# Lane inversions from VectorE to GpSimd, and the second half's statistics cut into three stages

## The chip, the cores and the metric

The kernel runs on one core of a Trainium2 chip. The metric is the device time of one launch in microseconds (us). The engines are named as in the profile: PE is TensorE's matmul side and PEld its weight load, DVE is VectorE, ACT is ScalarE, POOL is GpSimd, SP is SyncE, which issues the DMAs of this kernel. Each engine works through its own queue in order, and waits on semaphores that other engines and DMAs raise. Differences under 0.2% of the time (2.8 us) count as no change.

## The reference, cut to what matters

One layer of a hybrid decoder on x of 1024 tokens by 1024 channels, float32. The mixer normalises x, multiplies it by one projection, and splits the columns among a gated unit (A), a recurrent block (B) and RWKV-7 time mixing (C); then comes the output projection, and a gated feed-forward network with a final norm. What matters here is C, whose state is updated token by token:

```
def step(state, inp):
    r_t, w_t, k_t, v_t, kk_t, a_t = inp
    sa = jnp.einsum('bhvk,bhk->bhv', state, kk_t)
    state = (state * w_t[:, :, None, :]
             - sa[..., :, None] * (kk_t * a_t)[..., None, :]
             + v_t[..., :, None] * k_t[..., None, :])
    return state, jnp.einsum('bhvk,bhk->bhv', state, r_t)
```

and the norm in front of the mixer:

```
y = xf * lax.rsqrt(jnp.mean(xf * xf, axis=-1, keepdims=True) + EPS)
```

## The kernel before

The tokens are done in two halves of 512. For each half the six heads of C are done as three pairs, so there are six units of time mixing, called 00, 10, 20, 01, 11 and 21 (pair, half). Every product with a weight is three matmuls of 512 columns per 128 rows of the contraction (high and low parts of weight and activation, `gemm`).

The step above is done in chunks of 64 tokens. Within a chunk it needs the inverse of a triangular 64x64 matrix. One unit has 8 chunks and 2 heads, so 16 such matrices, and its work is cut into stages:

- `P` (function `rwkv`, up to its last `yield`): projections of k, r and v, then the matmuls `pg` (L624), from which DVE writes the matrices into `AK` (L628); SP stores them to the scratch `dA` in DRAM (L637).
- `L` (function `lanes`): SP loads the 64 diagonal 16x16 blocks of the unit back as `LA` (L668), one block to a partition; 15 steps of elimination follow, each a product into `LT` (L673) and a subtraction from `LX` (L675), on 8 to 36 elements a partition, and a negation (L676). These 31 instructions, each of which needs the one before, are called a lane here. SP stores the result (L679) and loads the whole matrices back into `AK` (L682).
- `M` (function `chain`): four DVE transposes `X` (L695), the matmuls `pz` and `py` (L690), which put the 16x16 inverses together to 64x64, and then the 8 chunks one after the other (matmuls `q`, L743).
- `E` (function `finish`): norm, gate and store of the unit's output `o`, with the transposes `po` (L783) on PE.

Beside them stand `B` and `R` (the recurrent block), `U` (the gated unit, whose values `pzt`, `sv` and gates `pu` appear below), `X` (inputs `xwa`, `xg`), `M` without digits (`macc`: one block of the modulation vector, multiplied on ACT and added on POOL), `S` (function `stats1`: sums of squares of the second half, their matmuls `pss`, the reciprocal root `rsq_n` on DVE, and its broadcast `pb_n` on PE, L266) and `H1` (the normalised second half, `h10` to `h17`). After the mixer come the output projection (`out_tile`, matmuls into `po`, L246 to L248) and the feed-forward network.

The order of the stages is the text `ORDER`: each word calls the next stage of a generator. Inside that, a scheduler that runs when the kernel is built orders the instructions of each engine by its own idea of when each can start; so a change of an instruction's engine also moves others. The engine for many elementwise steps comes from the table `ENG` through `eng()`; the lane is not in it. Of the PSUM pool `mp` there are three buffers, which `pss`, `pb`, `pg`, `pzt`, `pix`, `pz` and others take in turn.

Three names for stretches of PE's program: a unit's head runs from its last `pg` to its first `pz`, and holds the lane and the DMAs around it; its body runs from there to the next unit's last `pg`; behind the sixth `pz` comes the tail, up to the transposes `po` of unit 21.

Of the kernel before, what the change touches and what calls it, by code (L numbers as in the profile page):

```python
# [14 lines left out]
ALU = mybir.AluOpType  # L15
# [3 lines left out]
P = 128  # L19
D = 1024  # L20
S = 1024
# [100 lines left out]
H2N = (4, 4)  # L122
MODN = 10
XB = 2
ORDER = """X0*2 P00*3 S L00 B00 M U0 L00 M U0 M R00
M00*3 P10 M00 P10 M M00 P10 L10 M E00 R00 U0 M R00 E00 L10 B10 M R00 U0
M10*3 P20 M10 P20 M M10 P20 L20 M E10 R10*2 M E10 B20 R10*2 L20 M R20*4
M20 H1*2 M20*2 H1*2 X1 M X1 P01 M20 P01 M M20 P01 L01 M E20*2 L01 B01 M U1 R01
# [21 lines left out]
def trunk(ctx: ExitStack, tc: tile.TileContext, xT, wmod, w_in, w_out, w_up, w_down,  # L150
          par, const, sgu_ln, sgu_wT, sgu_b, lora, g2w, lruw, outT):
    nc = tc.nc
    V, A, G, T = (Ordered(tc, e) for e in (nc.vector, nc.scalar, nc.gpsimd, nc.tensor))
# [56 lines left out]
    def rsqrt(v, n, nm):  # L210

        t = cp.tile([P, 3, 16], F32, tag="rsq", name=f"rsq_{nm}", bufs=3)
        y, h, u = t[:, 0, 0:n], t[:, 1, 0:n], t[:, 2, 0:n]
        yi = y.bitcast(I32)
        V.tensor_single_scalar(yi, v.bitcast(I32), 1, ALU.arith_shift_right)
        V.tensor_scalar(yi, yi, -1.0, float(0x5F3759DF), ALU.mult, ALU.add)
        V.tensor_scalar(h, v, -0.5, None, ALU.mult)
        for _ in range(3):
            V.tensor_tensor(u, y, y, ALU.mult)
            V.tensor_tensor(u, u, h, ALU.mult)  # L220
            V.scalar_tensor_tensor(y, u, 1.5, y, ALU.add, ALU.mult)
        return y

    def eng(key, d):
        return {"V": V, "G": G, "A": A}[ENG.get(key, d)]
# [21 lines left out]
            T.matmul(ps, hi[k], al, start=False, stop=False)  # L247
            T.matmul(ps, lo[k], ah, start=False, stop=(k == len(acts) - 1))  # L248

    def sumsq_bcast(acc, psp, pool, tag, nm, bufs, direct=False):  # L250

        pss = psp.tile([P, H], F32, tag="m", name=f"pss_{nm}")
        for i, a in enumerate(acc):
            for j in range(4):
                T.matmul(pss[:, j:j + 1], a[:, j * P:(j + 1) * P], ones, start=(i == 0 and j == 0),
                         stop=(i == len(acc) - 1), skip_group_check=True)
        return rstd_bcast(pss, psp, pool, tag, nm, bufs, direct)

    def rstd_bcast(pss, psp, pool, tag, nm, bufs, direct=False):

        v = cp.tile([P, 4], F32, tag="rsv", name=f"rsv_{nm}", bufs=2)
        V.tensor_scalar(v, pss[:, 0:4], 1.0 / D, EPS, ALU.mult, ALU.add)
        r = rsqrt(v, 4, nm)
        pb = psp.tile([P, H], F32, tag="m", name=f"pb_{nm}")
        for j in range(4):
            T.matmul(pb[:, j * P:(j + 1) * P], r[:, j:j + 1].broadcast_to([P, P]), ident, start=True, stop=True)  # L266
        if direct:
            return pb
        rb = pool.tile([P, H], F32, tag=tag, name=f"rb_{nm}", bufs=bufs)
        A.copy(rb, pb)  # L270
        return rb
# [30 lines left out]
    mp = ctx.enter_context(tc.tile_pool(name="mp", bufs=3, space=PSUM))  # L302
# [27 lines left out]
    with tc.tile_pool(name="st", bufs=1, reuse_waits="tile") as st:  # L330
# [88 lines left out]
        mod_load(1)  # L419
        mod_ap(0)  # L420
        rb = sumsq_bcast([sacc], mp, st, "rb", "n10", 1)
        mod_v(0, 0, 8)
        w_load(0)
# [29 lines left out]
    r2 = r2s.enter_context(tc.tile_pool(name="r2", bufs=1, reuse_waits="tile"))  # L453
# [62 lines left out]
    def t2(nm):  # L516
        return r2.tile([P, H], F32, tag="t2", name=nm, bufs=NT2)

    def tb(nm):
        return r2.tile([P, H], F32, tag="tb", name=nm, bufs=NTB)  # L520
# [5 lines left out]
    def c_tile(f, wi, idx, o, nm):  # L526

        if f == 0 and wi in first:
            ps = first[wi]
        else:  # L530
            wt = load_w(w_in[wi], f"{nm}{f}")
            ps = acp.tile([P, H], F32, tag="acc", name=f"pc_{nm}{f}")
            gemm(ps, wt, acts[f])
        mu = col("rwkv_mu", idx)
        A.activation(o, ps, AF.Copy, scale=omu[:, idx:idx + 1])
        V.scalar_tensor_tensor(o[:, 1:H], ps[:, 0:H - 1], mu, o[:, 1:H], ALU.mult, ALU.add)
        if f == 0:
            A.copy(cryC[:, idx:idx + 1], ps[:, H - 1:H])
        else:
            V.scalar_tensor_tensor(o[:, 0:1], cryC[:, idx:idx + 1], mu, o[:, 0:1], ALU.mult, ALU.add)  # L540
        return o
# [5 lines left out]
    def rwkv(j, f, stages):  # L547
# [67 lines left out]
        r = c_tile(f, 3 + 3 * j, j, t2(f"r{n}"), f"r{j}")  # L615
# [35 lines left out]
        v = c_tile(f, 4 + 3 * j, 6 + j, t2(f"v{n}"), f"v{j}")  # L651
# [9 lines left out]
        def lanes():  # L661

            LA = r2.tile([P, 16, 16], F32, tag="LA", name=f"LA{n}", bufs=2)
            LX = r2.tile([P, 8, 16], F32, tag="LX", name=f"LX{n}", bufs=2)
            LT = r2.tile([P, 128], F32, tag="LT", name=f"LT{n}", bufs=1)
            blk = dA.rearrange("c h (b x) -> (c h b) x", x=1040)[:, 0:1024].rearrange("u (s t) -> u s t", t=64)
            for qq in range(2):
                SY.dma_start(LA[64 * qq:64 * qq + 64], blk[:, 0:16, 0:16])  # L668
            eng("lx", "G").tensor_copy(LX.rearrange("p a b -> p (a b)"), ey)
            for i in range(15):  # L670
                m, w = i // 2 + 1, 15 - i
                tmp = LT[:, 0:m * w].rearrange("p (a b) -> p a b", b=w)
                V.tensor_tensor(tmp, LX[:, 0:m, i:i + 1].broadcast_to([P, m, w]),  # L673
                                LA[:, i:i + 1, i + 1:16].broadcast_to([P, m, w]), ALU.mult)
                V.tensor_tensor(LX[:, 0:m, i + 1:16], LX[:, 0:m, i + 1:16], tmp, ALU.subtract)  # L675
            V.tensor_scalar(LX, LX, -1.0, None, ALU.mult)  # L676
            yield
            for qq in range(2):
                SY.dma_start(blk[:, qq:16:2, 0:16], LX[64 * qq:64 * qq + 64])  # L679
            for hh in range(2):  # L680
                r_ = slice(64 * hh, 64 * hh + 64)
                SY.dma_start(AK[r_, :, 0, r_], dA[:, hh, 0:4096].rearrange("c (s t) -> s c t", t=64))  # L682
            yield
# [83 lines left out]
        def finish():  # L767
# [28 lines left out]
            yield  # L796

        stages.update({f"L{j}{f}": lanes(), f"M{j}{f}": chain(), f"E{j}{f}": finish()})
        yield

# [136 lines left out]
    rb1 = []  # L937

    def stats1():

        acc = r2.tile([P, H], F32, tag="o", name="sacc", bufs=1)
        for k in range(KT):
            x = tb(f"xs1{k}")
            SY.dma_start(x, xT[k * P:(k + 1) * P, H:S])
            A.activation(acc if k == 0 else x, x, AF.Square)
            if k:
                eng("st1", "G").tensor_tensor(acc, acc, x, ALU.add)
        rb1.append(sumsq_bcast([acc], mp, r2, "rb", "n11", 1))
        yield

    def h1_in():
# [9 lines left out]
    def x_in(f):  # L961
# [14 lines left out]
        yield  # L976

    stages = {"M": mods(), "S": stats1(), "H1": h1_in()}
    for f in range(2):
        stages[f"X{f}"] = x_in(f)  # L980
# [4 lines left out]
    V.on = VPIN > 0  # L985
    for nw, w in enumerate(ORDER.split()):
        if nw == VPIN:
# [60 lines left out]
    def h2_in(f, acc):  # L1048

        rb = sumsq_bcast(acc, mp, f1, "rb", f"n2{f}", 1)  # L1050
        yield
        hn = x1[f]
        sh = [modc[:, 24 + k:25 + k] for k in range(KT)]
        for q in range(4):
            for i, new in enumerate((hnew, hnew) if f == 0 else (anew, gnew)):
                k = q + 4 * i
                V.scalar_tensor_tensor(hn[k], hn[k], sg2[:, k:k + 1], rb, ALU.mult, ALU.mult)
                parts(f"{i + 1}{f + 1}", q, hn[k], new, sh[k])
                yield
        for q in range(4 * f):  # L1060
            b11, b21, b12, b22 = x1[0][q], x1[0][q + 4], hn[q], hn[q + 4]
            eng("T1", "V").tensor_tensor(b11, b12, b11, ALU.subtract)
            eng("T3", "G").tensor_tensor(b12, b22, b12, ALU.subtract)
            eng("T2", "V").tensor_tensor(b22, b22, b11, ALU.subtract)
            eng("T4", "G").tensor_tensor(b21, b21, b22, ALU.subtract)
            parts("T2", q, b22, anew, sh[q + 4])
            parts("T1", q, b11, anew)
            parts("T4", q, b21, gnew)
            yield
        for q in range(4 * f):  # L1070
            parts("T3", q, hn[q], anew, dsh[:, q:q + 1])
            yield
# [227 lines left out]
    for f in range(2):  # L1300
        acc = f1.tile([P, H], F32, tag="g0", name=f"sa3{f}", bufs=NAHEAD + 1)
# [102 lines left out]
```

## Time and profile before

| | us |
|---|---|
| median of 3 runs (1388.76 to 1389.72) | 1389.36 |
| the profiled execution's own time | 1389.59 |
| its span in the profile | 1387.8 |
| PE busy | 1256.2 (91%) |
| DVE busy | 914.4 (66%) |
| ACT busy | 584.0 (42%) |
| POOL busy | 413.3 (30%) |

The mixer and the modulation fill the first 600 us, the output projection runs to about 642 us, and the rest is the feed-forward network. PE is busy nearly everywhere, but a row's duration on PE also holds what the clock costs: the granted clock (PEclk) is 1.00 where TensorE has its higher level of 2.4 GHz, and 0.50 at 1.2 GHz; a stretch's mean lies between. In the section of rows below, the seven windows of the first group are, from the top: body 20, head 01, head 11, head 21, the tail, the stretch behind the tail, and the output projection.

### The profile page before, as it was taken

The numbers are of one execution on the slowest core, as the hardware profiler recorded it, in microseconds if no ns is written. First come the engines' busy times: TensorE is split into PE (matmuls) and PEld (weight loads), VectorE is DVE, ScalarE is ACT, GpSimd is POOL, SyncE is SP. The second block draws the span as 40 slices with busy tenths as digits, with TensorE's granted clock in tenths as the row PEclk, the third lists the DMA queues.
The fourth block names the chain that finished last, engine by engine and source line by source line (L and its number), as shares of the span: only waits on it lengthen the run. The fifth ranks groups of instructions, "written<-read, shape, count | busy, mean of one in ns | idle before, by whom it ended". The sixth has DMA issues, their size and how long they took to land. (4 is left out here: it accounts for less than half of the span.)

```text
span 1387.8 us, 18658 instructions
## 1 busy us (share of the span) xinstructions
PE 1256.2 (91%) x6948; PEld 1025.9 (74%) x6948; DVE 914.4 (66%) x1624; ACT 584.0 (42%) x1008; POOL 413.3 (30%) x337
## 2 busy tenths in 40 slices
PE   2778999978898979989878999999999999999996
PEld 2566878667686867768656778888888888888885
DVE  7968776765668584567898766666666575332566
ACT  3454654854655366333444334343343342110231
POOL 5683423306124220023466433323333200000000
PEclk9999999979999988899989999999999999999998
DMA  6554161433314243385412322222222374321213
GB/s 225 189 168 121 35 168 52 113 126 97 83 51 109 65 124 107 116 272 188 137 45 84 100 91 84 91 84 91 74 71 91 109 261 133 93 76 51 82 54 121
DMA packets 87498, 153.89 MB, mean 111 GB/s; under 512 B 37616, under 2 KB 39280, under 8 KB 87408
## 3 DMA queue, kind: packets, MB, share of 16 engines
q1 hardware_dynamic: 87408, 152.71, 35.3%
q8 instruction: 54, 0.88, 0.3%
q14 instruction: 36, 0.29, 0.1%
HBM read 126.60 MB, written 26.08 MB: 110 GB/s over the span
## 5 line engine op out<-in xcount | busy, mean ns | idle before, releaser
L1246 DVE SCALAR_TENSOR_TENSOR x<-pd,modc,x 128x512 f32<-128x512 f32 x80 | 59.5, 748 | 83.4 <-PE pd L248 83.3
L1293 POOL TENSOR_TENSOR x<-x,rb_n 128x512 f32<-128x512 f32 x2 | 3.0, 1520 | 218.2 <-ACT rb_n L270 218.2
L287 POOL TENSOR_TENSOR macc<-macc,wm 128x512 f32<-128x512 f32 x35 | 46.8, 1338 | 68.1 <-ACT wm L285 66.0
L228 ACT CAST wh_wd<-wr_wd 128x768 fp32r<-128x768 f32 (+2 forms) x32 | 21.7, 677 | 93.6 <-PE pd L247 92.2
L229 POOL TENSOR_TENSOR wl_wo<-wr_wo,wh_wo 128x1024 fp32r<-128x1024 f32 x9 | 22.0, 2445 | 113.3 <-DVE O L774 57.6
L1224 POOL TENSOR_TENSOR u<-u,g 128x512 f32<-128x512 f32 x21 | 27.7, 1321 | 92.6 <-ACT g L1147 92.6
L229 DVE TENSOR_TENSOR wl_ug<-wr_ug,wh_ug 128x1024 fp32r<-128x1024 f32 x22 | 28.9, 1318 | 34.3 <-ACT wh_ug L228 34.3
L755 DVE TENSOR_SCALAR U<-q,rn 128x64 f32<-128x64 f32 x48 | 13.4, 279 | 48.3 <-PE q L743 41.1
L624 PE MATMUL pg<-KGd,KB 128*128 128x128 f32 x192 | 31.1, 307 | 7.5 <-DVE KGd L609 5.0
L763 ACT COPY O<-q 128x64 f32<-128x64 f32 x48 | 10.1, 211 | 65.5 <-PE q L743 65.2
L228 ACT CAST wh_ug<-wr_ug 128x1024 fp32r<-128x1024 f32 x22 | 23.1, 1052 | 34.2 <-PE pA L1122 31.3
L743 PE MATMUL q<-SS,KGd 128*128 128x64 f32 x180 | 36.7, 287 | 0.0
L743 PE MATMUL q<-VV,SCd 128*128 128x64 f32 x192 | 35.0, 285 | 0.3
L1208 DVE TENSOR_TENSOR p<-p,pB 128x512 f32<-128x512 f32 x21 | 14.4, 685 | 31.0 <-PE pB L1123 31.0
L1147 ACT ACTIVATE g<-g 128x512 f32<-128x512 f32 x44 | 27.9, 634 | 14.8 <-DVE g L1142 14.8
L624 PEld LDWEIGHTS pg<-KGd,KB 128*128 128x128 f32 x192 | 27.2, 215 | 9.0 <-DVE KGd L609 5.7
L228 ACT CAST wh_wo<-wr_wo 128x1024 fp32r<-128x1024 f32 x16 | 16.7, 1047 | 38.8 <-PE po L247 30.9
L743 PEld LDWEIGHTS q<-VV,SCd 128*128 128x128 f32 x192 | 29.9, 202 | 4.1 <-ACT O L763 1.4
L1140 DVE SCALAR_TENSOR_TENSOR g<-pA,pr,g 128x511 f32<-128x511 f32 (+1 forms) x42 | 31.2, 742 | 2.4 <-ACT g L1138 2.2
L1140 DVE SCALAR_TENSOR_TENSOR g<-p,pr,g 128x511 f32<-128x511 f32 (+1 forms) x42 | 32.1, 764 | 0.9 <-ACT g L1138 0.9
L285 ACT ACTIVATE wm<-wm,cs 128x512 f32<-128x512 f32 x35 | 24.1, 718 | 15.3 <-DMA wm<-in_wmod_dram 9.3
L1201 POOL TENSOR_TENSOR wr_ug<-wr_ug,wr_uv 128x512 f32<-128x512 f32 x18 | 29.7, 1651 | 1.4
(5041 smaller groups left out, 4574.1 us busy)
## 6 DMA issues: line engine op xcount, KB each, us to landing
wm<-in_wmod_dram SPq DMA_DIRECT2D x48, 512.0 KB, 4.1
wr_ug<-in_w_up_dram SPq DMA_DIRECT2D x22, 512.0 KB, 3.6
wr_uv<-in_w_up_dram SPq DMA_DIRECT2D x22, 512.0 KB, 3.6
wr_g<-gd SPq DMA_DIRECT2D x22, 512.0 KB, 3.5
x<-in_xT_dram SPq DMA_DIRECT2D x32, 256.0 KB, 5.2
wr_wo<-in_w_out_dram SPq DMA_DIRECT2D x16, 512.0 KB, 4.3
wr_wd<-in_w_down_dram SPq DMA_DIRECT2D x16, 384.0 KB, 3.0
gd<-c SPq DMA_DIRECT2D x21, 256.0 KB, 2.0
```

The lines of the kernel that those rows point to most:

```text
L228: A.copy(hi, src)
L229: (e or V).tensor_tensor(lo, src, hi.bitcast(F32), ALU.subtract)
L285: A.activation(acc if k == 0 else wt[:, j, :], wt[:, j, :], AF.Copy, scale=cs[:, k:k + 1])
L287: G.tensor_tensor(acc, acc, wt[:, j, :], ALU.add)
L624: T.matmul(pg[hh][:, c, :, :], KB[:, 4 * g + c, :, :].rearrange("p a b -> p (a b)"), KG[g][:, c, :, r_], start=True, stop=True)
L743: T.matmul(o, w, x, start=start, stop=True, skip_group_check=True)
L1140: V.scalar_tensor_tensor(g[:, d:H], src[:, 0:H - d], taps[2 - d], g[:, d:H], ALU.mult, ALU.add)
L1147: A.activation(g, g, AF.Silu)
L1201: eng("S4" + e, "G").tensor_tensor(g1, g1, v1, ALU.subtract)
L1208: V.tensor_tensor(self.p1, self.p1, psB, ALU.add)
L1224: eng("c22", "V").tensor_tensor(u3, u3, g1_, ALU.mult)
L1246: V.scalar_tensor_tensor(x, ps, modc[:, 40 + k:41 + k], x, ALU.mult, ALU.add)
```

## The change

The 31 instructions of each lane go from DVE to POOL, 186 in all. `stats1`, until now one stage, becomes three: the sums; the matmuls `pss` with the reciprocal root; the broadcast. In `ORDER` the single `S` becomes three, and the first goes behind the first `L00`. For this the function `rstd_bcast` is cut, and `sumsq_col` holds its first part.

```
-ORDER = """X0*2 P00*3 S L00 B00 M U0 L00 M U0 M R00
+ORDER = """X0*2 P00*3 L00 S B00 M U0 L00 S M U0 M S R00
...
-    def sumsq_bcast(acc, psp, pool, tag, nm, bufs, direct=False):
+    def sumsq_col(acc, psp, nm):

         pss = psp.tile([P, H], F32, tag="m", name=f"pss_{nm}")
...
-        return rstd_bcast(pss, psp, pool, tag, nm, bufs, direct)
-
-    def rstd_bcast(pss, psp, pool, tag, nm, bufs, direct=False):
-
         v = cp.tile([P, 4], F32, tag="rsv", name=f"rsv_{nm}", bufs=2)
         V.tensor_scalar(v, pss[:, 0:4], 1.0 / D, EPS, ALU.mult, ALU.add)
-        r = rsqrt(v, 4, nm)
+        return rsqrt(v, 4, nm)
+
+    def sumsq_bcast(acc, psp, pool, tag, nm, bufs, direct=False):
+
+        return rstd_bcast(sumsq_col(acc, psp, nm), psp, pool, tag, nm, bufs, direct)
+
+    def rstd_bcast(r, psp, pool, tag, nm, bufs, direct=False):
+
         pb = psp.tile([P, H], F32, tag="m", name=f"pb_{nm}")
...
-                V.tensor_tensor(tmp, LX[:, 0:m, i:i + 1].broadcast_to([P, m, w]),
+                G.tensor_tensor(tmp, LX[:, 0:m, i:i + 1].broadcast_to([P, m, w]),
                                 LA[:, i:i + 1, i + 1:16].broadcast_to([P, m, w]), ALU.mult)
-                V.tensor_tensor(LX[:, 0:m, i + 1:16], LX[:, 0:m, i + 1:16], tmp, ALU.subtract)
-            V.tensor_scalar(LX, LX, -1.0, None, ALU.mult)
+                G.tensor_tensor(LX[:, 0:m, i + 1:16], LX[:, 0:m, i + 1:16], tmp, ALU.subtract)
+            G.tensor_scalar(LX, LX, -1.0, None, ALU.mult)
...
-        rb1.append(sumsq_bcast([acc], mp, r2, "rb", "n11", 1))
+        yield
+        sums = sumsq_col([acc], mp, "n11")
+        yield
+        rb1.append(rstd_bcast(sums, mp, r2, "rb", "n11", 1))
         yield
```

What this does to PE's program: counted in matmuls of 512 columns, the six heads held 105, 112, 90, 107, 117 and 91, and hold 98, 102, 86, 72, 86 and 84 now. The five bodies held 46, 50, 108, 56 and 40, and hold 49, 68, 109, 63 and 64. In the tail stand 87 such matmuls where there were 58, and 12 more are left behind it. The head of unit 01, on PE, before (`pz01` is its first `pz`, `pc_r11` and `pc_k11` are projections of the next unit):

```order
L247 MATMUL pc_r11_3526<-h14l_2659,wh_r11_3522 128x512
L248 MATMUL pc_r11_3526<-h14h_2658,wl_r11_3521 128x512
L690 MATMUL pz01_3238<-X101_3232,AKd1_122 32x16 x32
L246 MATMUL pc_r11_3526<-h15h_2665,wh_r11_3522 128x512
L247 MATMUL pc_r11_3526<-h15l_2666,wh_r11_3522 128x512
```

and now:

```order
L246 MATMUL pc_k11_3418<-h11h_2579,wh_k11_3414 128x512
L247 MATMUL pc_k11_3418<-h11l_2580,wh_k11_3414 128x512
L693 MATMUL pz01_3238<-X101_3232,AKd1_122 32x16 x32
L248 MATMUL pc_k11_3418<-h11h_2579,wl_k11_3413 128x512
L246 MATMUL pc_k11_3418<-h12h_2586,wh_k11_3414 128x512
```

The `pz` that stood behind 14 of the 24 products of r now stands behind 5 of the 24 products of k, 35 matmuls of the head earlier.

On POOL the end of the first lane, now (`wl_k` is the low part of the weight of k for unit 10, `macc` the modulation, `LX_2219` the identity for a later lane, `wl_r` the low part of r's weight):

```order
L678 TENSOR_TENSOR LX_745<-LX_745,LT_746 128x7x3
L229 TENSOR_TENSOR wl_k_1198<-wr_k_1197,wh_k_1199 128x1024
L676 TENSOR_TENSOR LT_746<-LX_745,LA_744 128x14
L678 TENSOR_TENSOR LX_745<-LX_745,LT_746 128x7x2
L676 TENSOR_TENSOR LT_746<-LX_745,LA_744 128x8
L678 TENSOR_TENSOR LX_745<-LX_745,LT_746 128x8
L679 TENSOR_SCALAR LX_745<-LX_745 128x128
L290 TENSOR_TENSOR macc_852<-macc_852,wm_3_1375 128x512 x2
L672 COPY LX_2219<-cst 128x128
L229 TENSOR_TENSOR wl_r_1306<-wr_r_1305,wh_r_1307 128x1024
```

One wide product has got into the lane, and the POOL work that stood free before waits behind its end. In the same way two additions to `macc` stand inside the lane of unit 01, and one wide product in that of unit 11.

On SP the store and load behind the lane of unit 11, before:

```order
L679 DMA dA11_3587<-LX11_3696 64x8x16 x2
L523 DMA yd_108<-xr01_3174 128x512
L281 DMA wm9_1_4488<-in_wmod_dram 128x1024
L682 DMA AKd0_121<-dA11_3587 64x8x64 x2
L238 DMA wr_xr21_4508<-in_w_in_dram 128x1024
```

and now:

```order
L682 DMA dA11_3587<-LX11_3696 64x8x16
L685 DMA AKd0_121<-dA11_3587 64x8x64
L526 DMA yd_108<-o01_3855 128x512
L685 DMA AKd0_121<-dA11_3587 64x8x64
L238 DMA wr_v21_4368<-in_w_in_dram 128x1024
```

Two transfers that stood between store and load are gone, and one store of an earlier unit's output has come between the halves of the load. For units 10 and 21 nothing stands between any more (before: two transfers each); for unit 20 the load of the weight of `xg` does.

## Rows read from the trace of the kernel before

**Rows 1.** Windows: length; PE, PEld, DVE, ACT, POOL busy (count); PEclk; DMA share; GB/s.
```profile
277.30:344.30 67.00, 52.41 (x450) 44.44 (x449) 40.52 (x70) 34.42 (x62) 21.02 (x18) 0.85 0.35 113
344.30:381.00 36.70, 32.55 (x156) 24.86 (x154) 23.60 (x75) 22.85 (x39) 7.19 (x5) 1.00 0.33 85
413.20:458.80 45.60, 39.94 (x192) 30.83 (x193) 33.68 (x105) 20.50 (x38) 19.52 (x12) 0.93 0.45 120
487.60:531.10 43.50, 36.31 (x182) 27.89 (x180) 35.71 (x91) 26.17 (x45) 7.39 (x3) 0.88 0.43 120
531.10:578.60 47.50, 43.97 (x388) 36.25 (x387) 22.32 (x54) 23.68 (x46) 2.41 (x1) 0.78 0.28 89
578.60:598.80 20.20, 12.43 (x54) 9.40 (x54) 11.38 (x18) 9.60 (x17) 0.00 (x0) 0.95 0.78 251
598.80:641.70 42.90, 42.42 (x184) 34.42 (x184) 25.45 (x35) 11.70 (x15) 12.21 (x5) 0.95 0.74 246
```

**Rows 2.** Waits of PE, 60 to 620 us: in total, times, longest.
```profile
PE po L783 <- DVE LX L675: 5.3, 3, 4.0
PE pb_n L266 <- DVE rsq_n L221: 3.6, 1, 3.6
```

**Rows 3.** Windows of the six lanes, first to last instruction, all work (columns of rows 1).
```profile
115.60:127.20 11.60, 8.02 (x29) 6.49 (x28) 10.84 (x42) 4.80 (x7) 4.95 (x3) 0.71 0.29 93
184.00:197.50 13.50, 13.19 (x70) 10.33 (x70) 13.19 (x56) 7.88 (x12) 0.00 (x0) 1.00 0.45 137
253.20:264.80 11.60, 11.05 (x48) 8.18 (x48) 10.89 (x52) 10.60 (x15) 2.07 (x2) 1.00 0.17 50
355.40:371.80 16.40, 13.38 (x62) 9.74 (x60) 14.89 (x58) 10.12 (x17) 2.60 (x2) 1.00 0.32 101
426.90:447.20 20.30, 15.00 (x72) 11.72 (x71) 20.30 (x76) 8.66 (x13) 9.86 (x6) 0.98 0.32 105
500.30:520.20 19.90, 12.71 (x49) 8.93 (x50) 19.62 (x63) 14.04 (x20) 5.49 (x2) 0.78 0.38 133
```

**Rows 4.** Timeline of POOL: start, us, instruction; each needs the one before.
```profile
68.67 0.20 POOL L146 TENSOR_TENSOR spt<-spt 128x3 f32<-128x3 f32 x1
68.96 0.23 POOL L146 TENSOR_SCALAR spt<-spt 128x3 f32<-128x3 f32 x1
```

**Rows 5.** Timeline, POOL and DVE side by side inside the first lane.
```profile
117.64 2.34 POOL L229 TENSOR_TENSOR wl_k<-wr_k,wh_k 128x1024 fp32r<-128x1024 f32 x1 [2.71 <-ACT wh_k L228]
117.69 2.33 DVE L675 TENSOR_TENSOR LX<-LX,LT 128x24 f32<-128x24 f32 x1
```

**Rows 6.** The same windows, instructions that touch LT alone.
```profile
115.60:127.20 11.60, 9.72 (x30) 0.71 0.29 93
184.00:197.50 13.50, 5.44 (x30) 1.00 0.45 137
253.20:264.80 11.60, 6.87 (x30) 1.00 0.17 50
355.40:371.80 16.40, 5.39 (x30) 1.00 0.32 101
426.90:447.20 20.30, 10.93 (x30) 0.98 0.32 105
500.30:520.20 19.90, 9.60 (x30) 0.78 0.38 133
```

**Rows 7.** Timeline of DVE behind the lane of unit 20 (columns of rows 4).
```profile
273.41 0.44 DVE L695 STREAM_TRANSPOSE X<-AKd 32x256 f32<-32x256 f32 x1
```

**Rows 8.** SP's issues around the lanes of units 01 and 11, and landing times.
```profile
347.74 1.31 SPq L668 DMA_DIRECT2D LA<-dA  x2
...
447.26 2.57 SPq L679 DMA_DIRECT2D dA<-LX  x2
...
451.45 0.60 SPq L682 DMA_DIRECT2D AKd<-dA  x1
...
LA<-dA SPq DMA_DIRECT2D x12, 64.0 KB, 4.5
```

## The prediction

> **What bounds the kernel now.** I read the page's busy shares first: PE is busy 91% of the span, so nothing but PE's own time, its gaps and its clock can move the end by much. Then I read windows by stage [rows 1]. The feed-forward network behind 641.7 us has the same instructions in both kernels and is left out. In the mixer the reader is to see heads that last longer than PE's work in them: head 21 lasts 43.5 us with PE busy 36.3, at a mean clock of 0.88; head 11 lasts 45.6 with 39.9. PE runs its program in order, so a `pz` waits for its whole chain: last `pg`, write to DRAM, load `LA`, lane, store, load, `X`. Work of PE stands in between, and part of it waits too: PE waited 5.3 us in `po` for the lane's subtractions on DVE, which have nothing to do with `po` and only stood ahead of its producer in DVE's queue, and 3.6 us in `pb_n` for the reciprocal root, which DVE did among the first lane's steps [rows 2]. The windows of the lanes [rows 3] show 11.6, 13.5, 11.6, 16.4, 20.3 and 19.9 us, 93.3 in all. In the last two DVE was busy from end to end, 20.30 of 20.3 and 19.62 of 19.9: there the lane is as long as it is because DVE does other work between its steps.
>
> **The lane's price on POOL.** The trace has no lane on POOL, so it is bounded. Two dependent small instructions on POOL start 0.29 us apart [rows 4]; that is 8.7 us for 30. They have 3 elements a partition, the lane's 8 to 36, 24.8 on average (worked out from the loop). A wide product takes 2.34 us for 1024 elements [rows 5], 2.3 ns each, so 21.8 more cost 0.05 us, 1.5 over 30. The negation of 128 elements is 0.6 by the same two rows. Together 10.8 us, an estimate. On DVE the 30 products and subtractions took 5.39 to 5.44 us of busy time where nothing stretched them [rows 6], 0.18 each; POOL is thus not faster by itself.
>
> What it gains is a queue of its own, unless DVE's work gets in its way. In rows 5 a DVE instruction of 24 elements took 2.33 us beside a POOL product of 2.34, and ended with it; alone such an instruction takes 0.18. The one stood still for the other. With lanes on POOL it can be the lane that stands still. DVE's other work inside the lanes, rows 3 less rows 6, is 1.1, 7.8, 4.0, 9.5, 9.4 and 10.0 us, 41.8 in all. The bounds are none of it (the two never meet) and all of it (every DVE instruction stops the lane). I take half: a step that meets a running DVE instruction waits only for what is left of it. POOL's own work that now stands inside a lane is known: one wide product in the lane of 00 (2.3), two additions in 01 (2.6, the POOL rows of [rows 3]), one wide product in 11 (2.4).
>
> Lanes: 10.8 + 0.5 + 2.3 = 13.6; 10.8 + 3.9 = 14.7; 12.8; 10.8 + 4.7 + 2.6 = 18.1; 10.8 + 4.7 + 2.4 = 17.9; 15.8. That is 92.9 against 93.3: the lanes get longer by 2.0, 1.2, 1.2 and 1.7 in the first four, and shorter by 2.4 and 4.1 in the last two. The bounds for the sum are 72.1 (none) and 113.9 (all).
>
> The Trainium skill, "SBUF — State Buffer", section "Who interferes with whom", says that VectorE and GpSimd share a pair of ports under an exclusive lock, which a VectorE instruction with two inputs in SBUF takes against a GpSimd instruction that reads SBUF, the later one standing still until the first is through. Rows 5 agree (2.33 beside 2.34). By that rule alone, most of DVE's work in the lanes counts in full, which lies nearer to the upper bound; that is the slower rival below.
>
> **Heads.** A head is set by its chain, so a lane's change goes to it, plus what else moves. Head 00: lane +2.0; the wait in `pb_n` of 3.6 goes, but it hid under the chain, so +2.0. Head 10: +1.2, less 1.3 for two transfers that no longer stand between store and load (the price is that of head 11, below): -0.1. Head 20: its last `X` was done at 273.8 [rows 7] and its first `pz` ran at 277.3, where the window of body 20 begins [rows 1], a slack of 3.5 that takes the +1.2: 0. Head 01: +1.7, but its head starts about 2.5 us nearer the lane, since the issue of `LA` came at 347.74 and a landing takes 4.5 [rows 8], so data were there at about 352.5 to 353.5 while DVE began at 355.4: -0.8. Head 11: -2.4, and from the store's issue at 447.26 to the load's at 451.45 [rows 8] it took 4.2, with two transfers between; the store's own row is 2.57 long, so without them 2.9, an estimate: -1.3, together -3.7. Head 21: -4.1, and -1.3 for two transfers: -5.4. Sum -8.0.
>
> **Bodies and tail.** PE's matmuls are redistributed, not saved: 94 fewer in heads, 53 more in bodies, 41 more behind. In a head bound by its chain they were cover, so they cost in the bodies what they take: 42.42 us for 184 [rows 1], 0.23 each, 12.2 us for 53. Of these 21 lie ahead of body 20, which lasted 67.0 us with PE busy 52.4: it waits for inputs of the second half, and takes most of the 21's 4.8 us, say 4.5. Bodies: +7.7. In the tail, 47.5 us long, PE was busy 43.97 at a mean clock of 0.78, which is 34.3 at full clock. With 29 matmuls more (6.7) that is 41.0, if the dense work between the small `q` matmuls holds the clock at the upper level; with the tail's own idle 3.5 it would last 44.5: -3.0. At the old mean clock it would last 41.0 / 0.78 + 3.5 = 56, that is +8.6; I take the first because heads 01 (1.00) and 11 (0.93), where such matmuls stand, show the higher clock. The last 12 matmuls fall behind the tail into 20.2 us with PE busy 12.4 [rows 1]: nothing.
>
> **Three-part S.** It costs no instruction. Its sums and root no longer stand ahead of the first lane, and its matmuls take a buffer of `mp` earlier; behind it PE waits at the next `pix` for a buffer instead. Between nothing and the 3.6 of [rows 2]; I take nothing, since head 00 is bound by its chain.
>
> **Sum.** -8.0 + 7.7 - 3.0 = -3.3. The profiled execution took 1389.59 (span 1387.8 and 1.8 around it), 0.2 above the median. So 1386.3, or 1386.1 against the median: I say 1386.2.
>
> **Rivals.**
> *Slower: the port.* Lanes on POOL pay all of DVE's work. Against my half that is +0.5, +3.9, 0 (2.0, under the slack of 3.5), +4.8, +4.7 and +5.0, together +18.9: 1405. With three quarters it is half of that: 1396. It decides from about +1.3 us a lane on. For it: rows 5. Against it: before, POOL was busy only 25 of the 93 us of these windows [rows 3], so a step that is held up delays nothing behind it at once.
> *Faster: no meeting.* If the lanes run at 10.8 plus POOL's own work, heads fall by 0.5, 3.9, 0, 4.7, 4.7 and 5.0 more: -18.8, 1367.5; with a quarter of DVE's work in the way, 1377. For it: POOL is a free queue, and DVE, busy 20.30 of 20.3, sheds 31 instructions a unit, so its own producers (`O`, `o`, `xr`) come sooner. Against it: body and tail take what heads give back once PE has no cover.
> *No change.* PE's busy time is the same 1256 us; if what PE no longer waits for in `po` it waits for in `pz`, and the tail's clock stays as it was, the terms cancel: -8.0 + 7.7, 1389.1.
> If body 20 hides nothing, that term alone adds 4.5 to the forecast, 1390.7, which its own range holds.
>
> **How the numbers follow.** Chances: forecast 0.43, its own range 1380 to 1393; no change 0.12; slower port 0.23; faster 0.22. A difference under 0.2%, 2.8 us, can't be told from none: faster is below 1386.6. The forecast gives 0.22 faster, 0.14 same, 0.07 slower; no change 0.10 same and 0.01 on each side; the others fall whole on their sides. Sum 0.45, 0.24, 0.31. The range is 1371 to 1402: it leaves out the ends of both port cases, some 0.07 on each side.
>
> **What would show it.** In the changed profile: lanes on POOL of 13.6, 14.7, 12.8, 18.1, 17.9 and 15.8 us, by units; DVE rows of two inputs stretched beside them or POOL's rows at 0.3; no wait of `po` or `pb_n` for DVE's lane rows, but waits of PE at `pz` in heads 01, 11 and 21 of some 10 us; the tail at a clock near 1.00; 2.9 us from the store's to the load's issue in unit 11. The forecast is wrong if the lanes are under 12 us where DVE is busy, or over 20, if PE has work enough that `pz` no longer waits, or if the tail's clock falls to where 87 matmuls last longer than 47.5 us.

## The result, and the profile after

The changed kernel takes 1396.29 us (median of 7, 1391.63 to 1398.02) against 1388.76 for the one before (7 runs): ratio 1.0051, interval 1.0032 to 1.0070. It is slower by half a per cent; 1386.2 was forecast. On another chip it gave 1.0070 (1.0055 to 1.0086). Its profiled execution took 1394.93, with a span of 1393.2, 5.4 longer than before; its mean clock of 0.952 is the highest of the seven (the others have 0.944 to 0.950), so the profile shows less of the loss than the medians do.

The six lanes came out shorter in sum than the 92.9 us of the forecast. Windows of the six lanes in the profile after, instructions that touch `LT` alone (length, POOL busy, PEclk, DMA share, GB/s); they answer to [rows 3, 6]:

```profile
109.80:122.00 12.20, 7.09 (x30) 1.00 0.23 58
182.80:195.30 12.50, 9.14 (x30) 1.00 0.33 106
264.30:278.20 13.90, 10.99 (x30) 1.00 0.10 38
361.70:376.90 15.20, 9.97 (x30) 0.94 0.23 70
435.20:448.50 13.30, 8.10 (x30) 1.00 0.25 79
506.90:520.70 13.80, 10.87 (x30) 1.00 0.33 110
```

Read the lengths against those of [rows 3]: 80.9 us in all, 12.4 less. But the first three last 38.6 where they lasted 36.7; the whole gain is in the last three, 42.3 instead of 56.6.

Where the time went shows in the windows by stage. First the stages of the kernel before that [rows 1] doesn't have: head 00, body 00, head 10, body 10, head 20, body 01, body 11.

```profile
100.90:140.50 39.60, 34.36 (x154) 26.43 (x153) 32.55 (x90) 18.22 (x32) 15.12 (x11) 0.91 0.47 125
140.50:169.50 29.00, 27.30 (x349) 23.10 (x349) 22.41 (x38) 18.97 (x39) 11.78 (x12) 1.00 0.13 38
169.50:209.90 40.40, 38.81 (x227) 31.09 (x226) 29.35 (x81) 20.63 (x42) 13.44 (x10) 1.00 0.57 161
209.90:239.60 29.70, 29.20 (x362) 25.06 (x362) 17.17 (x37) 15.44 (x35) 7.61 (x9) 1.00 0.13 38
239.60:277.30 37.70, 34.75 (x167) 25.74 (x166) 27.60 (x79) 30.18 (x52) 14.54 (x11) 0.95 0.41 106
381.00:413.20 32.20, 31.67 (x378) 27.23 (x378) 21.87 (x43) 17.52 (x36) 6.53 (x8) 1.00 0.16 51
458.80:487.60 28.80, 27.66 (x357) 23.77 (x357) 17.25 (x38) 12.68 (x30) 7.28 (x8) 1.00 0.13 38
```

After, the six heads and bodies in the order of time, then the tail and the stretch behind it:

```profile
96.40:137.70 41.30, 30.76 (x147) 23.53 (x145) 22.30 (x57) 17.02 (x30) 22.09 (x41) 0.90 0.44 113
137.70:169.80 32.10, 30.10 (x354) 25.17 (x353) 21.97 (x38) 19.05 (x39) 12.37 (x12) 0.92 0.12 34
169.80:205.30 35.50, 34.76 (x202) 27.63 (x201) 23.85 (x47) 18.80 (x39) 18.83 (x39) 1.00 0.45 125
205.30:248.90 43.60, 37.72 (x397) 32.20 (x395) 21.41 (x40) 18.39 (x42) 11.17 (x11) 0.92 0.23 73
248.90:287.40 38.50, 30.37 (x148) 22.68 (x147) 24.08 (x46) 30.08 (x49) 23.75 (x41) 0.98 0.36 100
287.40:354.30 66.90, 57.37 (x461) 48.78 (x462) 42.59 (x71) 34.17 (x63) 22.72 (x19) 0.78 0.36 116
354.30:386.10 31.80, 26.37 (x124) 19.54 (x123) 18.54 (x40) 16.02 (x30) 15.11 (x35) 0.94 0.34 81
386.10:420.50 34.40, 34.03 (x377) 28.77 (x378) 22.43 (x44) 21.15 (x43) 10.23 (x9) 0.95 0.15 48
420.50:458.10 37.60, 31.17 (x169) 24.10 (x171) 28.07 (x72) 19.23 (x37) 24.88 (x42) 0.94 0.43 117
458.10:495.70 37.60, 36.67 (x386) 31.34 (x387) 18.45 (x39) 14.19 (x32) 8.61 (x9) 0.88 0.19 58
495.70:531.90 36.20, 31.34 (x154) 23.55 (x156) 26.38 (x58) 22.81 (x39) 17.92 (x34) 0.91 0.43 109
531.90:580.80 48.90, 46.42 (x431) 38.67 (x429) 27.55 (x58) 25.72 (x51) 2.41 (x1) 0.90 0.35 115
580.80:602.70 21.90, 16.80 (x65) 12.82 (x65) 12.38 (x19) 11.10 (x18) 0.00 (x0) 0.92 0.68 224
```

Summed: the stretch up to the first head is 4.5 shorter, the heads 22.6 shorter (243.5 to 220.9), the bodies 27.9 longer (186.7 to 214.6), the tail 1.4, the stretch behind it 1.7, all the rest 1.5 longer: +5.4. By halves, from the last `pg` of unit 00 to that of unit 01 it takes 257.9 instead of 243.4 (+14.5), and from there to `po` of unit 21 226.5 instead of 234.3 (-7.8). The column to read in the bodies is the clock: 1.00, 1.00, 0.85, 1.00, 1.00 before, and 0.92, 0.92, 0.78, 0.95, 0.88 after.

PE's waits, 60 to 650 us (in total, times, longest). Of those in [rows 2] the one of `po` for the lane is gone and that of `pb_n` is down to 0.4, and these stand in their place:

```profile
PE pix L828 <- DVE sv L898: 9.9, 1, 9.9
PE pz L693 <- DVE X L698: 9.8, 3, 6.0
PE py L693 <- DVE X L716: 7.5, 2, 3.9
```

The first of them from DVE's side. After 120.73 the next work for `sv` was ready, but `X` stood ahead of it, and DVE sat idle for 8.99 us until the load of `AKd` landed:

```profile
120.73 0.17 DVE L890 BATCH_NORM_AGGREGATE smv<-sbs 128x2 f32<-128x6 f32 x1
...
129.88 0.43 DVE L698 STREAM_TRANSPOSE X<-AKd 32x256 f32<-32x256 f32 x1 [8.99 <-DMA AKd<-dA]
```

The wait at `py` in unit 10, on ACT and on SP. ACT had the chain's copy to `AKd` behind a product of the modulation whose load had not landed; that load was issued at 208.32, behind the chain's:

```profile
207.79 0.21 ACT L754 COPY Y<-q 128x64 f32<-128x64 f32 x1
211.85 0.72 ACT L288 ACTIVATE wm<-wm,cs 128x512 f32<-128x512 f32 x1 [3.85 <-DMA wm<-in_wmod_dram]
```

```profile
198.23 1.27 SPq L685 DMA_DIRECT2D AKd<-dA  x2
...
208.32 1.65 SPq L284 DMA_DIRECT2D wm<-in_wmod_dram  x2
```

And what the clock did behind it, body 10 cut into the stretch up to the end of that wait, the next 7.5 us, and the rest (columns of rows 1). PE was busy 4.0 of 8.5 us, then 7.5 of 7.5 at a mean clock of 0.55, then at 1.00 again:

```profile
205.30:213.80 8.50, 4.04 (x146) 3.30 (x144) 4.36 (x5) 4.34 (x11) 2.53 (x2) 1.00 0.77 239
213.80:221.30 7.50, 7.50 (x78) 5.82 (x79) 0.28 (x1) 2.78 (x6) 0.00 (x0) 0.55 0.04 14
221.30:248.90 27.60, 26.18 (x174) 23.08 (x172) 16.77 (x34) 11.26 (x25) 8.64 (x9) 1.00 0.12 39
```

### The profile page after: what moved, and what is told of

Its sections match the earlier page's. It is cut to its first block, busy times and chain, and to the rows that moved or that the text cites. A ratio compares the mean times of both kernels' runs of the same rounds, so it can differ in the third digit from the quotient of the medians.

```text
span 1393.2 us, 18660 instructions
## 1 busy us (share of the span) xinstructions
PE 1256.7 (90%) x6948; PEld 1027.1 (74%) x6948; DVE 881.7 (63%) x1438; ACT 580.8 (42%) x1006; POOL 469.5 (34%) x523
## 5 line engine op out<-in xcount | busy, mean ns | idle before, releaser
L229 DVE TENSOR_TENSOR wl_ug<-wr_ug,wh_ug 128x1024 fp32r<-128x1024 f32 x22 | 28.9, 1318 | 34.3 <-ACT wh_ug L228 34.3
L676 POOL TENSOR_TENSOR LT<-LX,LA 128x30 f32<-128x30 f32 (+10 forms) x90 | 29.9, 332 | 21.2 <-DMA LA<-dA 14.7
L1153 ACT ACTIVATE g<-g 128x512 f32<-128x512 f32 x44 | 27.9, 634 | 14.5 <-DVE g L1148 14.5
L1146 DVE SCALAR_TENSOR_TENSOR g<-p,pr,g 128x511 f32<-128x511 f32 (+1 forms) x42 | 32.1, 765 | 0.9 <-ACT g L1144 0.9
L698 DVE STREAM_TRANSPOSE X<-AKd 32x256 f32<-32x256 f32 x24 | 10.4, 435 | 31.5 <-DMA AKd<-dA 31.0
```

The lines of the kernel that those rows point to most:

```text
L229: (e or V).tensor_tensor(lo, src, hi.bitcast(F32), ALU.subtract)
L1146: V.scalar_tensor_tensor(g[:, d:H], src[:, 0:H - d], taps[2 - d], g[:, d:H], ALU.mult, ALU.add)
```

## The experiments

Each ratio is to the kernel before on the same chip. The kernels came in groups, each group on a chip of its own: e_lanes to e_early, e_modv to e_p2, e_sv to e_best, e_hb to e_after, e_fill, and e_last. In this order the median of before was 1387.5, 1388.6, 1392.3, 1386.2, 1390.0 and 1396.4, and its mean clock 0.952, 0.952, 0.954, 0.954, 0.953 and 0.951. Times of different groups therefore can't be compared in us; the ratios can, and an expectation in us is meant for a before of about 1389.

| kernel | us | ratio (95%) | mean clock |
|---|---|---|---|
| e_lanes | 1397.9 | 1.0073 (1.0049 to 1.0096) | 0.947 |
| e_s | 1388.7 | 1.0000 (0.9978 to 1.0021) | 0.952 |
| e_hold | 1405.5 | 1.0126 (1.0095 to 1.0158) | 0.951 |
| e_early | 1384.9 | 0.9975 (0.9956 to 0.9993) | 0.953 |
| e_modv | 1389.5 | 1.0006 (0.9983 to 1.0029) | 0.946 |
| e_bmodv | 1376.9 | 0.9922 (0.9902 to 0.9943) | 0.956 |
| e_p1 | 1402.4 | 1.0105 (1.0083 to 1.0127) | 0.945 |
| e_p2 | 1381.6 | 0.9940 (0.9919 to 0.9960) | 0.952 |
| e_sv | 1394.8 | 1.0021 (1.0007 to 1.0034) | 0.950 |
| e_u00 | 1397.9 | 1.0029 (1.0015 to 1.0042) | 0.949 |
| e_u10 | 1400.1 | 1.0057 (1.0036 to 1.0077) | 0.946 |
| e_best | 1381.8 | 0.9928 (0.9902 to 0.9954) | 0.957 |
| e_hb | 1398.3 | 1.0079 (1.0053 to 1.0105) | 0.944 |
| e_hbc | 1394.0 | 1.0069 (1.0048 to 1.0089) | 0.949 |
| e_habc | 1392.9 | 1.0052 (1.0033 to 1.0071) | 0.950 |
| e_after | 1395.7 | 1.0070 (1.0055 to 1.0086) | 0.947 |
| e_fill | 1399.4 | 1.0083 (1.0053 to 1.0113) | 0.957 |
| e_last | 1387.8 | 0.9933 (0.9909 to 0.9957) | 0.956 |

**Which part: the lanes or S, and is it PE's order?** My first theory was that the matmuls taken out of the heads cost the time.

e_lanes, the lanes' edit alone. 

> Lanes on POOL, S in one stage and in its old place. PE's order is then that of the changed kernel in all heads but for two or three matmuls (heads 525 matmuls of 512 columns, bodies 354; before 619 and 301). Order theory (the time goes because 94 matmuls leave the heads for the bodies and the tail, so PE waits in the heads and starts the bodies at the lower clock): 1394 to 1397. Theory of S (PE waits 9.85 us at pix in head 00 for DVE's sv, because S no longer lies there): 1386 to 1390. POOL theory (lanes on POOL hold up DVE's and POOL's other work, whatever the order): 1394 to 1397.

e_s, the edit of S alone. 

> S in three stages, lanes on DVE. PE's order is that of before (heads 616, bodies 304). Order theory and POOL theory: 1388 to 1390. Theory of S: 1393 to 1396.

e_hold is the changed kernel with an order edge for five units, so that `pz` stands on PE where it stood before:

```
+HOLD = {"00": ("r10", 5), "10": ("k20", 13), "01": ("r11", 14), "11": ("v21", 13), "21": ("yg21", 16)}
...
+    for n, (g, i) in HOLD.items():
+        tc.add_manual_dep(PZ[n].ins, GM[g][i].ins.name, ...)
```

> The changed kernel, with the first pz of units 00, 10, 01, 11 and 21 held on PE behind the matmul that stood ahead of it before (heads 626, bodies 294). Order theory: below before, 1380 to 1388, since the lanes stay 12 us shorter in sum and the cover is back. POOL theory and theory of S: 1394 to 1398.

e_early turns it round on the kernel before: matmuls of the next unit wait in PE's queue for `pz`.

```
+        tc.add_manual_dep(GM[g + f][i].ins, PZ[n].ins.name, ...)
```

> The kernel before, lanes on DVE, with matmuls of the next unit held on PE behind the first pz, so that pz stands about where the changed kernel has it (heads 556, bodies 342). Order theory: slower than the changed kernel, 1397 to 1408, since the lanes last 93 us in sum instead of 81. POOL theory and theory of S: 1388 to 1392.

The lanes are all of it (1.0073), S is nothing. The order theory fell from both sides: PE's order of before under lanes on POOL made it slower (1.0126), and `pz` early under lanes on DVE made it no slower (0.9975). PE's order by itself isn't the loss.

**Is it the modulation on POOL, and which lanes?**

e_modv and e_bmodv:

```
-MODAP = (4, 5, 6, 7, 8)
+MODAP = ()
```

> The changed kernel with the modulation of blocks 4 to 8 on DVE alone (one multiply-add for each half of a load, as block 9 has it before and after) instead of multiplied on ACT and added on POOL. Theory of the modulation (on POOL the additions macc now stand behind the lanes; the load buffers wm come free late, the next loads land late, and ACT, which waits 36.2 us for them instead of 9.3, holds the chain's copies of AKd and Z behind that wait): that wait goes, and the time falls by 7 or more against the changed kernel, to 1380 to 1389. Theory of the shared port (lanes on POOL and DVE's two-input work hold each other up): DVE has some 30 us more of such work, 1394 to 1404.

> The same edit on the kernel before, lanes on DVE: DVE has both. Theory of the modulation: nothing is gained here, since no lane stands ahead of macc on POOL, and DVE's lanes get longer: 1388 to 1400. If it is as fast as the other one with this edit, the edit helps by itself and not by the lanes.

e_p1 and e_p2 (and e_u00, e_u10 with one unit):

```
+            LE = G if n in ("00", "10", "20") else V
             for i in range(15):
...
-                G.tensor_tensor(tmp, LX[:, 0:m, i:i + 1] ...
+                LE.tensor_tensor(tmp, LX[:, 0:m, i:i + 1] ...
```

> The changed kernel with the lanes of units 00, 10 and 20 on POOL, those of 01, 11 and 21 on DVE. By the trace the changed kernel is 10 us behind at the end of body 20, so all theories that put the loss into the first half's bodies: 1394 to 1399. Theory of the shared port, by which the late lanes (most of DVE's work beside them) lose most: 1388 to 1392.

> The other half: lanes of units 01, 11 and 21 on POOL, the first three on DVE. By the trace the changed kernel makes up 8 of its 10 us from head 01 to the tail: loss in the first half's bodies: 1379 to 1386, faster than before. Theory of the shared port: 1392 to 1397.

Moving the modulation to DVE gains 0.8% on the kernel before, against my expectation; the changed one comes to 1.0006, a gain of 0.45 to 0.65% beside its ratios on other chips. Between the two the lanes on POOL still cost 0.8%. So additions that queue behind lanes are not the cause. In e_modv ACT has no products of the modulation either, and yet body 10 (the stretch that the profile after shows at 0.92) ran at a clock of 0.87, with 1.8 us as PE's longest wait:

```profile
206.30:246.10 39.80, 38.00 (x395) 33.37 (x388) 21.99 (x44) 14.64 (x36) 10.08 (x9) 0.87 0.26 80
```

The halves tell it: the first three lanes on POOL cost 1.05%, the last three gain 0.6%, and the two add up to the change. With S alone at 1.0000, that is the lanes' doing. It also goes against the shared port, by which the last three, with most of DVE's work beside them, would lose most.

**Where in the first half?**

e_sv, an order edge on DVE: `X` of unit 00 behind `sv`. 

> The changed kernel, with the four transposes X of unit 00 held on DVE behind the two products sv of the gated unit. In the changed kernel DVE sat idle for 8.99 us at X (the load of AKd was not there), with the work for sv ready behind it, and PE waited 9.9 us at pix for sv. Theory of DVE's order (the scheduler put X too early, since it takes a lane on POOL to be over sooner than it is; the gap and the lower clock behind it are the loss): 1385 to 1391, with that wait under 3 us. Theory of the matmuls in the bodies (body 10 and body 20 are the loss, whatever head 00 does): 1393 to 1397.

e_u00: 

> The changed kernel with the lane of unit 00 alone on POOL. Theory of DVE's order: most of the loss of the first half is here, 1395 to 1400. Theory of the matmuls in the bodies: 1388 to 1392.

e_u10: 

> The changed kernel with the lane of unit 10 alone on POOL. Theory of DVE's order: 1386 to 1391. Theory of the matmuls in the bodies (this lane moves 16 matmuls of head 10 into body 10, and there ACT waits for a load of the modulation ahead of the copies of AKd): 1394 to 1399.

The ratios of 1.0029 and 1.0057, on a before of 1388.8, are 1392.8 and 1396.7 us: e_u00 lies between the two theories, and e_u10 where that of the matmuls had it. But the two are not the prices of one unit each, since their second half moved too, though its lanes stand on DVE as before: body 11, 28.8 us at a clock of 1.00 before (28.9 at 1.00 in e_p1), is here, in e_u00 and in e_u10,

```profile
464.20:496.30 32.10, 30.97 (x344) 27.28 (x342) 16.40 (x37) 12.99 (x31) 6.54 (x8) 0.79 0.07 19
```

```profile
464.60:497.70 33.10, 32.33 (x344) 28.82 (x345) 16.01 (x37) 12.98 (x31) 6.13 (x8) 0.74 0.06 18
```

In e_sv the wait at `pix` fell from 9.9 to 4.4 us, not under 3, and body 00 from 32.1 to 30.1; the ratio of 1.0021 stands beside 1.0051 and 1.0070 for the changed kernel on other chips. Body 10 with unit 10's lane on DVE (e_u00), and on POOL (e_u10), nearly the same PE instructions:

```profile
213.20:249.60 36.40, 34.69 (x396) 30.07 (x395) 20.32 (x40) 16.77 (x39) 8.64 (x9) 1.00 0.22 73
```

```profile
203.70:249.30 45.60, 39.39 (x394) 33.47 (x395) 22.94 (x42) 18.82 (x42) 11.21 (x11) 0.85 0.22 75
```

9.2 us longer: 4.7 of PE's busy time, which is the clock of 0.85, and 4.5 of waiting.

**Mending the queues.** Order edges on the changed kernel, one place more each time (the lines of four kernels put together; the comments say which has them):

```
+    pairs += [(I["X", "00", q], I["sv", 0]) for q in range(4)]              # e_habc, e_last
+    pairs += [(I["wm", 6, k], I["AK2", "10"]) for k in range(4)]            # all four
+    pairs += [(I["h", 1, 0], I["AK", "20"])]                                # e_hbc, e_habc, e_last
+    pairs += [(I["wm", m, k], I["AK2", "10"]) for m, k in ((5, 6), (5, 7))] # e_last
...
+    for late, early in pairs:
+        tc.add_manual_dep(late.ins, early.ins.name, ...)
```

> The changed kernel, with the modulation's four products of block 6 that stand on ACT among the copies of unit 10's chain (Z, AKd) held behind them. There ACT waited 3.85 us for a load of the modulation, and PE 3.59 at py behind it. Theory of waiting heads of queues (an instruction that waits for something late stands ahead of the chain's next step, or the chain's step ahead of ready work): body 10 shorter by 4 to 8 us, ratio to before down by 0.002 to 0.005 against the changed kernel. Theory of the matmuls in the bodies: no change in the ratio.

> As the one before, and the first product h10h of the second half's input held on ACT behind the copies of AKd of unit 20 (there ACT waited 3.35 us for DVE's x, and PE 3.86 at py). Theory of waiting heads of queues: a further 2 to 5 us. Theory of the matmuls in the bodies: no change.

> As the one before, and the transposes X of unit 00 held on DVE behind sv, which alone brought the ratio to 1.0021. Theory of waiting heads of queues: all three places mended, the lanes' shorter time is left over: ratio 0.993 to 0.999, 1380 to 1388. Theory of the matmuls in the bodies: 1.002 or more.

> The changed kernel again, on the chip of these runs, as the measure for the three others: ratio 1.003 to 1.007 by every theory.

> The changed kernel with the holds of e_habc, and two more products of the modulation (block 5) held on ACT behind unit 10's chain. In e_habc ACT waited 7.2 us for that load ahead of Z, PE waited 2.9 us at pz behind it, and the clock was at 0.50 for the next 10 us of body 10, which lasted 41.4 us with the same 395 matmuls that took 36.4 at full clock where the lane of unit 10 was on DVE. Theory of the modulation's loads (they now stand on SP behind the load of AKd, land late, and ACT's products stand ahead of the chain): body 10 falls to 36 to 39 us at a clock of 0.95 or more, and the ratio to 1.000 to 1.004. If the wait only moves to another place of the chain: body 10 stays above 40, ratio 1.004 to 1.007.

In e_hb body 10 of the profiled execution fell to 36.7 us at a clock of 1.00, as expected, with waits of 1.2 and 1.4 us left in it:

```profile
205.10:241.80 36.70, 34.05 (x397) 29.98 (x395) 20.93 (x40) 18.76 (x42) 12.62 (x11) 1.00 0.28 87
```

That execution (1391.25 us, clock 0.952) was one of the two fastest of six; over all runs the ratio didn't move (1.0079 beside 1.0070 for e_after on the same chip), and the mean clock was the lowest of all, 0.944. e_hbc brings 1.0069 and all three holds together 1.0052; the intervals part none of them from e_after. In e_habc the wait had moved one step up the chain: ACT waited 7.2 us for another load of the modulation, with the copy to `Z` behind it. e_last holds that too, and is faster than before on its chip: 0.9933. Its 1387.8 us are 8 below the changed kernel on two other chips; the changed kernel wasn't run on this one, whose median of before (1396.4) is the highest of the six, at the lowest clock. The expectation for body 10 failed in its profiled execution: the wait was gone (1.06 us at `pz` is what was left), yet the clock fell all the same, and the body lasted 41.9:

```profile
195.00:206.90 11.90, 10.86 (x60) 8.68 (x59) 5.66 (x11) 4.19 (x7) 3.60 (x12) 1.00 0.30 67
206.90:210.00 3.10, 3.08 (x137) 2.92 (x138) 3.10 (x4) 0.64 (x3) 0.00 (x0) 0.67 0.45 156
210.00:226.00 16.00, 16.00 (x122) 12.95 (x122) 2.80 (x8) 5.77 (x16) 2.54 (x2) 0.64 0.39 122
226.00:248.80 22.80, 21.38 (x141) 18.93 (x139) 15.85 (x31) 11.09 (x23) 8.64 (x9) 1.00 0.14 47
```

That execution had a clock of 0.950 and 1391.1 us; the other seven had 0.953 to 0.960 and 1384.3 to 1389.6.

**Is it the clock?** On the chip of e_after the mean clock over all runs was 0.954 for the kernel before and 0.947 for the changed one. The difference of 0.007 over some 1390 us is 10 us, an estimate of what the lower level cost, and the change lost 9.5. It isn't so for every kernel: e_hold lost 18.0 us at 0.951 beside 0.952. e_fill adds matmuls that nothing reads where PE waited:

```
+FILL = {"pix00": (36, "k10", 21), "py10": (14, "k20", 3), "pz20": (22, "yg20", 23), "py20": (14, None, 0)}
...
+        FD[key] = [T.matmul(ps, lor[:, 0:P], acts[0][7][0], start=True, stop=True) for _ in range(FILL[key][0])]
```

> The changed kernel with 86 matmuls of 512 columns added on PE whose result nothing reads: 36 before pix of unit 00, 14 before py of unit 10, 22 before the first pz and 14 before py of unit 20, where PE waited 9.9, 3.6, 6.0 and 3.9 us. They are 20 us of work at 0.23 each. Clock theory (the granted clock falls behind these waits, and the bodies that now hold more matmuls run at it: 0.92, 0.92 and 0.78 in bodies 00, 10 and 20, at a cost of some 15 us): with PE kept busy the clock stays up, and the time falls by 5 to 12 us although work was added: ratio 0.998 to 1.003, mean clock of the run above 0.952. If the clock doesn't hang on these waits: nothing gained, and what overruns the waits is lost: ratio 1.007 to 1.015, mean clock 0.945 to 0.949.

The mean clock was 0.957 (0.947 for e_after, on another chip), and head 00 and body 00 ran at 1.00:

```profile
95.70:136.00 40.30, 36.61 (x171) 28.41 (x169) 21.36 (x57) 16.61 (x28) 21.19 (x40) 1.00 0.48 119
136.00:166.70 30.70, 29.57 (x370) 25.41 (x369) 24.06 (x43) 20.00 (x42) 15.25 (x13) 1.00 0.12 36
```

They last 71.0 together instead of 73.4, with 8 us of work more. In body 10 and body 20 the fill did little for the clock: 0.92 as without it, and 0.82 instead of 0.78:

```profile
205.60:247.90 42.30, 40.39 (x411) 34.57 (x412) 23.82 (x42) 18.82 (x42) 13.20 (x12) 0.92 0.25 76
286.20:354.30 68.10, 58.70 (x456) 49.98 (x445) 43.13 (x68) 36.22 (x66) 24.44 (x21) 0.82 0.34 112
```

The mean clock came out as the clock theory had it (above 0.952), the time did not (1.0083): 0.010 of 1397 us is 14 us, an estimate of what the clock gave back, and 20 us of work were added; head 10 also got longer (38.9 instead of 35.5). So around head 00 the low clock goes with the wait, and filling waits with work that isn't needed doesn't pay.

**A kernel that beats both.** 

> The lanes of units 01, 11 and 21 on POOL, the others on DVE, and the modulation on DVE alone: the two edits that gained (ratios 0.994 and 0.992). If they add up: 0.984 to 0.989, 1367 to 1374. If both live off the same room on DVE: 0.990 to 0.996.

 The two gains don't add: 0.9928. The modulation on DVE with the lanes left there (e_bmodv, 0.9922, 1376.9 us) beats both kernels; the intervals don't part it from e_best, e_last or e_p2.

## Why the prediction was wrong

*The lanes, right way, and further than forecast.* Forecast 92.9 us, measured 80.9, lower than the forecast for units 00, 10, 01, 11 and 21. The term that was mis-sized is DVE's work in their way. A step on POOL takes 0.24 us (median), and where nothing holds it up the next one follows 0.32 after it began, as in the first lane:

```profile
114.23 0.24 POOL L676 TENSOR_TENSOR LT<-LX,LA 128x32 f32<-128x32 f32 x1
114.55 0.26 POOL L678 TENSOR_TENSOR LX<-LX,LT 128x32 f32<-128x32 f32 x1
```

So 30 steps with the negation are 10.2 and six lanes 61; with POOL's own 7.5 inside, 12 of the 80.9 are left for DVE, an estimate, not half of 41.8. The 41.8 itself was too low. It is the covered time of all of DVE less that of the lane, and DVE's records overlap, as these of the lane of unit 10 in the kernel before do:

```profile
189.25 0.20 DVE L673 TENSOR_TENSOR LT<-LX,LA 128x36 f32<-128x36 f32 x1
189.37 0.16 DVE L219 TENSOR_TENSOR rsq_o<-rsq_o 128x8 f32<-128x8 f32 x1
189.48 0.20 DVE L675 TENSOR_TENSOR LX<-LX,LT 128x36 f32<-128x36 f32 x1
189.60 0.16 DVE L220 TENSOR_TENSOR rsq_o<-rsq_o 128x8 f32<-128x8 f32 x1
```

Counted by itself, DVE's other work covers 58.2 us of the six windows before, and DVE was busy for 59.3 us of the six windows now. So about a fifth of the work beside the lanes held them up. DVE's side shows no loss: up to the end of the output projection the same 760 instructions outside the lanes cover 407.0 us before and 405.5 now. The Trainium skill, "SBUF — State Buffer", section "Who interferes with whom", has either engine stand still for the other; the rows agree that both can (a step of the lane took up to 1.19 us on POOL, and [rows 5] has DVE's at 2.33). That most of DVE's work would count in full they don't bear out (12 of 59.3).

*The heads, right way.* Forecast -8.0, measured -22.6. Heads 10, 01, 11 and 21 fell by 4.9, 4.9, 8.0 and 7.3; PE had less work in them, and the chain came sooner.

*The bodies: the step that failed.* "In a head bound by its chain they were cover, so they cost in the bodies what they take: ... 0.23 each, 12.2 us for 53", and then 4.5 off for body 20: +7.7. Measured +27.9. The price of the work was about right: PE's busy time by the granted clock of each body is 160.4 us before and 171.7 after, +11.3. But 0.23 is the price at the full clock, and the bodies no longer ran at it: busy less that product is 7.9 before and 24.2 after, 16.3 us that no term had. The forecast weighed the clock in the tail alone; in the bodies it put a change of it at nothing without a reason. And body 20 hid nothing (66.9 after 67.0, though it starts 10 us later). That 1396.3 still lies inside the range of 1371 to 1402 is luck: the heads came out 14.6 us better than forecast, the bodies 20.2 and the tail 4.4 worse.

*What lies under it, as far as the trace shows.* I had put the stall of head 00 under S, "Between nothing and the 3.6", and took nothing. It was 9.9 us, and came with the lanes, not with S (e_lanes has it at 7.4, e_s not at all). In the chain of unit 10 I had priced the two transfers gone from between store and load as a gain of 1.3; the loads of the modulation stand behind the chain's load instead, land late, and hold ACT in front of the chain's copies. The waits of `po` for the lane and of `pb_n` went but for 0.4 us, as forecast, and others came at `pix`, `pz` and `py`. I had such waits at `pz`, about 10 us in heads 01, 11 and 21; there they are 1.6, 2.3 and none, and stand in units 00, 10 and 20 instead.

*The tail.* Forecast -3.0 at a clock near 1.00; measured +1.4 at 0.90, up from 0.78.

*The rivals.* The slower one named the time (1396) and not the cause: it wanted longer lanes. That the lanes got shorter, and the kernel slower, was in none of them. That the first three lanes had nothing to gain could be read: [rows 3] have them at 11.6 to 13.5 us, little above the 10.8 of a lane alone on POOL, and the two that I named as held up by DVE were the last.

*What stays open.* Shown is that the loss lies with the lanes of the first half, that S and PE's order alone don't make it, and that a lower clock comes with it, in the bodies and over all runs. What lowers it there is not shown. In units 00 and 10 the trace has waits at the head of DVE's and ACT's queues with the low clock behind them. Holding that of unit 00 brought 1.0021 on a chip where the changed kernel wasn't run; where it was, e_hb, e_hbc and e_habc don't part from it; the fourth hold (e_last) brought 0.9933, again without it beside. And in e_modv, where ACT's products are gone, body 10 has the low clock all the same. The clock of bodies 10 and 20 also differs between kernels with nearly the same program, and the mean clock between executions of one. Unit 20's own share wasn't run.

## What to carry to other kernels

Before moving a chain of small steps to an idle engine, ask of each place whether the old engine was the limit there: here it was in three lanes of six, and moving only those gained 0.6% where moving all lost 0.5%. Where a scheduler orders the queues, a shorter stage also moves what other engines have at the head of theirs; look at each in-order queue for an instruction that waits for a late transfer with the chain behind it, but measure before counting on the gain: here three such places mended brought nothing that the intervals part. Price work that loses its cover at the clock that it will get, not at the best one.

## What the runs showed of the hardware

A dependent step of 8 to 36 elements on POOL took 0.20 to 0.27 us where nothing held it up (first lane), and the next one came 0.28 to 0.35 us after it began; on DVE a step took 0.18. Beside some 59 us of work on DVE the six lanes on POOL lost about 12 us, an estimate, and DVE's own work showed no loss. In body 10 PE's clock fell behind waits of 3.59 us (0.55 over the next 7.5 us), of 2.9 (e_habc, 0.53 over 10.4) and of 1.06 (e_last, 0.64 to 0.67 over 19.1), although PE was busy nearly throughout these stretches; behind waits of 1.2 and 1.4 (e_hb) and of 0.6 (before) it stayed at 1.00. So the length of the wait alone doesn't tell.
